# Token-stationary matmuls for the gates and the branch products of a hybrid decoder layer

## The chip, the cores and the metric

The kernel runs on one core of one Trainium2 chip. The metric is the time of one execution on the device, in microseconds. The names of the engines in the profile are PE for TensorE's matmuls, PEld for its weight loads (which overlap the matmuls), DVE for VectorE, ACT for ScalarE, POOL for GpSimd and SP for SyncE, whose queue issues most of the DMAs. All arithmetic is done in 32-bit floats.

## What is computed

The reference is one layer for 256 tokens of width 2048. Cut to what this change touches, it reads:

```python
proj = x @ w_in                      # (256 x 2048) @ (2048 x 14,352); columns are split among the mixers
y_lru = rg_lru(...)                  # 256 x 1024
y_gla = rmsnorm(gla(...)) * silu(r)                  # r: 1024 columns of proj
y_dn  = rmsnorm(gated_deltanet(...)) * silu(z)       # z: 1024 columns of proj
gates = sigmoid(gate_logits.reshape(256, 3, 2048) + b_gate)     # 6144 columns of proj
merged = (gates[:, 0] * (y_lru @ w_branch[0]) + gates[:, 1] * (y_gla @ w_branch[1])
          + gates[:, 2] * (y_dn @ w_branch[2]))      # w_branch[b]: 1024 x 2048
x = LN(alpha * x + merged @ w_out)                   # w_out: 2048 x 2048
x = LN(alpha * x + relu(x @ w1 + b1)**2 @ w2 + b2)   # w1: 2048 x 8192, w2: 8192 x 2048
```

The change concerns r, z, the gate logits, the three branch products and the way that merged reaches the product with w_out.

## The kernel before

Each large product is computed to nearly full precision from three passes of a reduced 32-bit type: every operand is split into hi (ACT casts it) and lo = raw - hi (DVE subtracts, `split`, lines 93 to 96), and the sum hi·hi + hi·lo + lo·hi is accumulated in PSUM.

The work is a list of jobs (`run_jobs`). A job is one block of weights of 1 MB (128 x 2048 numbers; 512 KB for a branch product): its DMA on SP into one of three `raw` buffers, its split into `hi` and `lo` halves (three buffers of each), its matmuls, and the evacuation of the sums. Load and split of a job are written ahead of the matmuls of the job before it.

There are two forms of matmul. In the first (`jobB`, `mmB`, lines 121 to 140, and `job_branch`), a 128 x 128 tile of weights is the stationary operand and the 256 tokens are the moving one; the sum has channels in rows and is 128 x 256. A job of 16 contraction tiles has 48 such matmuls, a branch job 24. In the second (`jobs_gla_v`, `jobs_out`, the second MLP product), 128 tokens are stationary and 512 columns of weights move; the sum has tokens in rows and is 128 x 512. A job has 24 such matmuls.

The gate jobs (line 124 onwards, 16 for each branch b) and the branch jobs (lines 982 to 986, 16 for each) alternate; `evac_gate` applies tanh on ACT, `evac_branch` multiplies on DVE and adds into `mg` on POOL (line 882). `mg` has channels in rows, as the output projection (`jobs_out`, lines 915 to 917) wants it for its stationary operand, so that it is only split into `mh` and `ml`.

Beside the jobs run the mixers, written as generators (`gen_lru`, `gen_gla`, `gen_dn` and others): after each job `pump` takes steps from them up to a budget of DVE and ACT time. `gen_dn` inverts triangular matrices through a round trip in DRAM on POOL's DMA queue. A scheduler then sets the order of the instructions on each engine from data dependences; each engine runs its own list in that order. After the output projection the first layer norm is computed (`norm_stats`, lines 944 to 947), transposed on PE (`p_x`, line 1077) and fed to the first MLP product (`accH`, then `accB` of lines 124 to 127 again).

PSUM has four buffers for the jobs' sums (`mm`) and four for the mixers (`mx`).

## Time and profile before

| | before |
|---|---|
| three timed runs | 1744.10, 1744.58 (median), 1745.21 us |
| span of the profiled execution, first to last instruction | 1743.0 us |
| mean granted TensorE clock | 0.997 |
| instructions | 30,261 |
| DMA | 319.96 MB, mean 184 GB/s |

The time of the profiled execution as a whole is not listed apart; its span lies 1.1 to 2.2 us under the three runs, 1.58 us under their median. In the profile, the duration of a matmul reaches from its start to the modelled end of its drain, so that matmuls that follow each other overlap; the pace is read from the distance of two starts. A row "A <- B" says that A waited for B. The granted clock 1.00 is the upper of TensorE's two levels.

### The profile page before, as it was taken

How to read it: one execution, taken by the hardware profiler on the slowest of the kernel's cores; microseconds unless marked ns; L12 is line 12 of the kernel's file. 1: busy time of each engine (PE TensorE's matmuls, PEld its weight loads, DVE VectorE, ACT ScalarE, POOL GpSimd, SP SyncE). 2: the span in 40 equal slices, each digit the busy share in tenths (PEclk: the TensorE clock that was granted, in tenths of full speed). 3: DMA queues.
4: the chain of work that ended last, by engine and by line, in shares of the span. 5: the costliest groups of instructions: out<-in, count | busy, mean ns of one | idle time of the engine just before them, and what ended most of it. 6: DMA issues, size and time to landing. Idle time of an engine off the chain costs nothing.

```text
span 1743.0 us, 30261 instructions
## 1 busy us (share of the span) xinstructions
PE 1722.7 (99%) x12782; PEld 1644.9 (94%) x12782; DVE 1058.2 (61%) x1353; ACT 889.8 (51%) x1209; POOL 76.7 (4%) x112
## 2 busy tenths in 40 slices
PE   8999999999999999999999999999999999999997
PEld 8999898999999999999998899999999988888897
DVE  7876456876765585565555675444444455576767
ACT  6785445785344443444444455554545444455553
POOL 0000000000120203000000000000000000000000
PEclk9999999999999999999999999999999999999999
DMA  8445543444564446355566835555545455555552
GB/s 328 150 170 187 197 173 125 166 170 149 184 194 148 161 170 187 130 181 182 184 217 223 308 109 209 190 177 187 187 177 193 172 192 195 194 193 193 203 193 97
DMA packets 52536, 319.96 MB, mean 184 GB/s; under 512 B 6752, under 2 KB 7136, under 8 KB 18992
## 3 DMA queue, kind: packets, MB, share of 16 engines
q1 hardware_dynamic: 49280, 310.92, 50.3%
q0 software_dynamic: 2976, 6.84, 1.5%
q8 instruction: 100, 1.64, 0.4%
q14 instruction: 36, 0.29, 0.0%
q10 hardware_dynamic: 144, 0.26, 0.0%
HBM read 315.09 MB, written 2.88 MB: 182 GB/s over the span
## 4 chain that ended last, share of the span: by engine, by line
PE 97%; DVE 1%; DMA 1%; ACT 0%; issue 0%; SPq 0%; DVEq 0%
PE accB L124 19%; PE accB L127 19%; PE accB L125 19%; PE accM L1200 7%; PE accM L1201 7%; PE accM L1199 7%; PE accB L982 3%; PE accB L984 3%; PE accB L986 3%; PE accO L917 1%; PE accO L915 1%; PE accO L916 1%; PE accV L467 1%; PE accV L469 1%; PE accV L468 1%; DMA raw<-in_w_dram 0%
## 5 line engine op out<-in xcount | busy, mean ns | idle before, releaser
L95 DVE TENSOR_TENSOR lo<-raw,hi 128x1024 fp32r<-128x1024 f32 (+2 forms) x584 | 708.6, 1216 | 541.6 <-ACT hi L94 537.8
L94 ACT CAST hi<-raw 128x1024 fp32r<-128x1024 f32 (+2 forms) x584 | 602.4, 1034 | 757.1 <-PE accB L125 406.0
L124 PE MATMUL accB<-xh,hi 128*128 128x256 f32 x1744 | 431.0, 285 | 0.0
L125 PE MATMUL accB<-xl,hi 128*128 128x256 f32 x1744 | 427.9, 283 | 0.0
L124 PEld LDWEIGHTS accB<-xh,hi 128*128 128x128 f32 x1744 | 334.4, 192 | 2.4 <-issue 1.4
L125 PEld LDWEIGHTS accB<-xl,hi 128*128 128x128 f32 x1744 | 334.5, 192 | 0.4
L127 PE MATMUL accB<-xh,lo 128*128 128x256 f32 x1744 | 244.9, 283 | 0.0
L124 PE MATMUL accB<-x1h,hi 128*128 128x256 f32 x976 | 239.7, 283 | 0.0
L125 PE MATMUL accB<-x1l,hi 128*128 128x256 f32 x976 | 239.5, 283 | 0.0
L127 PEld LDWEIGHTS accB<-xh,lo 128*128 128x128 f32 x1744 | 225.0, 192 | 0.1
L1200 PE MATMUL accM<-hi,hl 128*128 128x512 f32 (+1 forms) x608 | 212.8, 350 | 0.0
L1199 PE MATMUL accM<-hi,hh 128*128 128x512 f32 (+1 forms) x608 | 212.8, 350 | 0.0
L1201 PE MATMUL accM<-lo,hh 128*128 128x512 f32 (+1 forms) x608 | 212.8, 350 | 0.0
L125 PEld LDWEIGHTS accB<-x1l,hi 128*128 128x128 f32 x976 | 187.4, 192 | 0.0
L124 PEld LDWEIGHTS accB<-x1h,hi 128*128 128x128 f32 x976 | 187.4, 192 | 0.0
L127 PE MATMUL accB<-x1h,lo 128*128 128x256 f32 x976 | 137.0, 283 | 0.0
L1199 PEld LDWEIGHTS accM<-hi,hh 128*128 128x128 f32 x608 | 115.1, 189 | 15.1
L1200 PEld LDWEIGHTS accM<-hi,hl 128*128 128x128 f32 x608 | 115.1, 189 | 15.0
L1201 PEld LDWEIGHTS accM<-lo,hh 128*128 128x128 f32 x608 | 115.1, 189 | 14.8
L127 PEld LDWEIGHTS accB<-x1h,lo 128*128 128x128 f32 x976 | 125.9, 192 | 0.0
L982 PE MATMUL accB<-yh,hi 128*128 128x256 f32 x384 | 109.8, 286 | 0.0
L986 PE MATMUL accB<-yh,lo 128*128 128x256 f32 x384 | 108.7, 283 | 0.0
(308 smaller groups left out, 1861.3 us busy)
## 6 DMA issues: line engine op xcount, KB each, us to landing
raw<-in_wB_dram SPq DMA_DIRECT2D x109, 1024.0 KB, 4.8
raw<-in_w_dram SPq DMA_DIRECT2D x64, 1024.0 KB, 4.8
raw<-in_w2a_dram SPq DMA_DIRECT2D x32, 1024.0 KB, 4.8
raw<-in_w2b_dram SPq DMA_DIRECT2D x32, 1024.0 KB, 4.8
raw<-in_wBr_dram SPq DMA_DIRECT2D x48, 512.0 KB, 3.4
raw<-in_wO_dram SPq DMA_DIRECT2D x16, 1024.0 KB, 4.9
raw<-in_wV_dram SPq DMA_DIRECT2D x8, 1024.0 KB, 4.8
raw<-in_xw_dram SPq DMA_DIRECT2D x15, 384.0 KB, 8.0
```

What stands on the lines that cost most here:

```text
L94: i1 = sc.copy(hi, raw)
L95: i2 = ve.tensor_tensor(lo, raw, hi.bitcast(F32), ALU.subtract)
L124: te.matmul(acc, lhsT=hi[:, k, :], rhs=rh[:, k, :], start=start and k == 0, stop=False)
L125: te.matmul(acc, lhsT=hi[:, k, :], rhs=rl[:, k, :], start=False, stop=False)
L127: te.matmul(acc, lhsT=lo[:, k, :], rhs=rh[:, k, :], start=False, stop=stop and k == 7)
L467: te.matmul(accs[nh][tt], lhsT=sh, rhs=hi, start=k == 0, stop=False)
L982: te.matmul(acc[:, :T], lhsT=job.hi[0][:, 4 * i + k, :], rhs=yh[b][i][:, k, :], start=i == 0 and k == 0, stop=False)
L984: te.matmul(acc[:, :T], lhsT=job.hi[0][:, 4 * i + k, :], rhs=yl[b][i][:, k, :], start=False, stop=False)
L986: te.matmul(acc[:, :T], lhsT=job.lo[0][:, 4 * i + k, :], rhs=yh[b][i][:, k, :], start=False, stop=i == 1 and k == 3)
L1199: te.matmul(t, lhsT=sh, rhs=hi, start=k == 0, stop=False)
L1200: te.matmul(t, lhsT=sl, rhs=hi, start=False, stop=False)
L1201: te.matmul(t, lhsT=sh, rhs=lo, start=False, stop=k == NK2 - 1)
```

## The change

Five groups of products take the second form: r (`accR`), z (`accZ`), the gate logits (`accG`) and the branch products (`accY`) join `accV` in one function, `jobs_tok`. For each branch b and block cb of 512 channels there are now four gate jobs and two branch jobs, each of 1 MB. The sums have tokens in rows, so the gate's bias differs along a row: it is fetched as a row, broadcast to 128 partitions by POOL's DMA queue (`load_bg`, one buffer), and added on DVE before the tanh. `mg` has tokens in rows, and `gen_merged` transposes it on PE, 32 transposes of 128 x 128 in all (`p_m`), before ACT and DVE split it. silu(r) and silu(z) are multiplied in before the transposes that the mixers had already; ACT then scales and casts straight from PSUM (`to_branch_scaled`). The activation `dummy`, which loads the table for the square root ahead of the norm, now reads the row of biases instead of `mg`. A branch of 16 gate and 16 branch jobs becomes 16 gate and 8 branch jobs.

```diff
@@ -330,6 +327,10 @@
+    def to_branch_scaled(src, g, hi, lo):
+        sc.activation(hi, src, AF.Copy, scale=g)
+        ve.scalar_tensor_tensor(lo, src, g, hi.bitcast(F32), ALU.mult, ALU.subtract)
...
         ve.scalar_tensor_tensor(dst, t, 1.0, acc, ALU.add, ALU.mult)
 
-    def evac_gla_r(k):
-        def f(acc):
-            if k % 4 == 0:
-                gla["r", k // 4] = b4_tile("rr", [P, 4, T])
-            silu2(acc, gla["r", k // 4][:, k % 4, :])
-            if k == 7:
-                live.append(gen_gla())
+    def jobs_tok(src, nkg, rows_of, evac, nm):
+        accs = []
+        jobs = []
+        for kg in range(nkg):
+            job = Job(src[kg], 16, None, None)
+            def mm(job=job, kg=kg):
+                if kg == 0:
+                    accs.extend(mm_tile(nm) for _ in range(NT))
+                for k4 in range(4):
+                    k = 4 * kg + k4
+                    hi = job.hi[k4 // 2].rearrange("p k c -> p (k c)")[:, (k4 % 2) * 512:(k4 % 2) * 512 + 512]
+                    lo = job.lo[k4 // 2].rearrange("p k c -> p (k c)")[:, (k4 % 2) * 512:(k4 % 2) * 512 + 512]
+                    rh, rl = rows_of(k)
+                    for tt in range(NT):
+                        sh, sl = rh[:, tt * P:(tt + 1) * P], rl[:, tt * P:(tt + 1) * P]
+                        te.matmul(accs[tt], lhsT=sh, rhs=hi, start=k == 0, stop=False)
+                        te.matmul(accs[tt], lhsT=sl, rhs=hi, start=False, stop=False)
+                        te.matmul(accs[tt], lhsT=sh, rhs=lo, start=False, stop=k == 4 * nkg - 1)
+                if kg == nkg - 1:
+                    for tt in range(NT):
+                        evac(tt, accs[tt])
+            job.mm = mm
+            jobs.append(job)
+        return jobs
+    def x_rows(k):
+        return xh[k // 8][:, k % 8, :], xl[k // 8][:, k % 8, :]
+    def evac_gla_v(nh):
+        def f(tt, acc):
+            if nh == 0:
+                gla["v", tt] = b4_tile(f"v{tt}", [P, 4, 256])
+            (sc.copy if tt else ve.tensor_copy)(
+                gla["v", tt].rearrange("p h c -> p (h c)")[:, nh * 512:(nh + 1) * 512], acc)
         return f
 
-    def jobs_gla_v():
...
+    def evac_silu(dic, nm, nh, after=None):
+        def f(tt, acc):
+            if nh == 0:
+                dic[nm, tt] = b4_tile(nm, [P, 1024])
+            t = t2_tile("th", [P, 512])
+            sc.activation(t, acc, AF.Tanh, scale=0.5)
+            ve.scalar_tensor_tensor(dic[nm, tt][:, nh * 512:(nh + 1) * 512], t, 1.0, acc, ALU.add, ALU.mult)
+            if nh == 1 and tt == NT - 1 and after:
+                live.append(after())
+        return f
 
     def gen_gla():
         yield None
...
@@ -552,8 +563,9 @@
         y_alloc(1)
         for h in range(4):
             for tt in range(NT):
-                ve.tensor_scalar(o[tt][:, h, :], o[tt][:, h, :], rs[:, tt, h:h + 1], None, ALU.mult)
-            yield (.6, 0)
+                ve.scalar_tensor_tensor(o[tt][:, h, :], o[tt][:, h, :], rs[:, tt, h:h + 1],
+                                        gla["r", tt][:, h * 256:(h + 1) * 256], ALU.mult, ALU.mult)
+            yield (.8, 0)
         yield None
         for h in range(4):
             p = mx_tile("p_got")
...
-                ve.scalar_tensor_tensor(y, p[:, a * T:(a + 1) * T], g4[:, a:a + 1], gla["r", k // 4][:, k % 4, :],
-                                        ALU.mult, ALU.mult)
-                to_branch(y, yh[1][k // 4][:, k % 4, :], yl[1][k // 4][:, k % 4, :])
-            yield (1.8, .9)
-    dn = {"qk": {}, "z": {}, "v": {}, "nv": 0}
+                to_branch_scaled(p[:, a * T:(a + 1) * T], g4[:, a:a + 1],
+                                 yh[1][k // 4][:, k % 4, :], yl[1][k // 4][:, k % 4, :])
...
@@ -840,6 +843,9 @@
         for tt in range(NT):
             ve.tensor_tensor(o[tt], o[tt], rs[:, tt, :].unsqueeze(2).to_broadcast([P, 8, P]), ALU.mult)
             yield (1.1, 0)
+            ov = o[tt].rearrange("p h c -> p (h c)")
+            ve.tensor_tensor(ov, ov, dn["dz", tt], ALU.mult)
+            yield (1.1, 0)
         yield None
         for hp in range(4):
             p = mx_tile("p_dot")
...
-                                        ALU.mult, ALU.mult)
-                to_branch(y, yh[2][k // 4][:, k % 4, :], yl[2][k // 4][:, k % 4, :])
-            yield (1.4, .9)
-    mg = []
+                to_branch_scaled(p[:, j * T:(j + 1) * T], g4[:, 2:3],
+                                 yh[2][k // 4][:, k % 4, :], yl[2][k // 4][:, k % 4, :])
+            yield (1, .9)
...
+    mg = {}
     mh, ml = [], []
-    def evac_gate(b, d):
-        def f(acc):
-            t = t1_tile("gate", [P, T])
-            sc.activation(t, acc, AF.Tanh, scale=0.5, bias=bgh[:, b * 16 + d:b * 16 + d + 1])
-            gates[b, d] = t
+    gates = {}
+    def load_bg(b, cb):
+        t = sm.tile([P, 512], F32, tag="bg", name="bgrow", bufs=1)
+        gp.dma_start(t, bg[b:b + 1, cb * 512:(cb + 1) * 512].to_broadcast([P, 512]))
+        gates["row"] = t
+    def evac_gate(b, cb):
+        def f(tt, acc):
+            t = t2_tile("gate", [P, 512])
+            ve.tensor_tensor(t, acc, gates["row"], ALU.add)
+            sc.activation(t, t, AF.Tanh, scale=0.5)
+            gates[tt] = t
         return f
 
-    gates = {}
-    def evac_branch(b, d):
-        def f(acc):
-            i, j = d // 4, d % 4
-            if b == 0 and d == 0:
-                mg.extend(b4_tile(f"mg{a}", [P, 4, T]) for a in range(4))
-            m = mg[i][:, j, :]
-            t = gates.pop((b, d))
+    def evac_branch(b, cb):
+        def f(tt, acc):
+            if b == 0 and cb % 2 == 0:
+                mg[tt, cb // 2] = b4_tile(f"mg{tt}", [P, 1024])
+            m = mg[tt, cb // 2][:, (cb % 2) * 512:(cb % 2) * 512 + 512]
+            t = gates.pop(tt)
             if b == 0:
                 ve.scalar_tensor_tensor(m, t, 1.0, acc, ALU.add, ALU.mult)
                 return
-            u = t1_tile("gb", [P, T])
-            ve.scalar_tensor_tensor(u, t, 1.0, acc, ALU.add, ALU.mult)
-            gp.tensor_tensor(m, m, u, ALU.add)
-            if b == 2 and j == 3:
-                mh.append(b4_tile(f"mh{i}", [P, 4, T], F32R))
-                ml.append(b4_tile(f"ml{i}", [P, 4, T], F32R))
-                to_branch(mg[i], mh[i], ml[i])
+            ve.scalar_tensor_tensor(t, t, 1.0, acc, ALU.add, ALU.mult)
+            gp.tensor_tensor(m, m, t, ALU.add)
+            if b == 2 and tt == NT - 1:
+                live.append(gen_merged(cb))
         return f
 
+    def gen_merged(cb):
+        mh.append(b4_tile(f"mh{cb}", [P, 4, T], F32R))
+        ml.append(b4_tile(f"ml{cb}", [P, 4, T], F32R))
+        yield None
+        for kp in range(2):
+            p = mx_tile("p_m")
+            for a in range(2):
+                c = (cb % 2) * 512 + (2 * kp + a) * P
+                for tt in range(NT):
+                    te.transpose(p[:, a * T + tt * P:a * T + (tt + 1) * P], mg[tt, cb // 2][:, c:c + P], ident)
+            pv = p.rearrange("p (a t) -> p a t", a=2)
+            hi, lo = mh[cb][:, 2 * kp:2 * kp + 2, :], ml[cb][:, 2 * kp:2 * kp + 2, :]
+            sc.copy(hi, pv)
+            ve.tensor_tensor(lo, pv, hi.bitcast(F32), ALU.subtract)
+            yield (.7, .7)
     xt = {}
@@ -963,44 +984,35 @@
         jobs.append(jobB(wB[17 + h], evac_gla_q(h)))
     for h in range(4):
         jobs.append(jobB(wB[21 + h], evac_gla_k(h)))
-    jobs += jobs_gla_v()
-    for k in range(8):
-        jobs.append(jobB(wB[25 + k], evac_gla_r(k)))
+    for nh in range(2):
+        jobs += jobs_tok(wV[nh], 4, x_rows, evac_gla_v(nh), "accV")
+    for nh in range(2):
+        jobs += jobs_tok(wR[nh], 4, x_rows, evac_silu(gla, "r", nh, gen_gla), "accR")
     for h in range(8):
-        jobs.append(jobB(wB[33 + 8 + h], evac_dn("k", h)))
-        jobs.append(jobB(wB[33 + h], evac_dn("q", h)))
+        jobs.append(jobB(wB[25 + 8 + h], evac_dn("k", h)))
+        jobs.append(jobB(wB[25 + h], evac_dn("q", h)))
     for h in range(8):
-        jobs.append(jobB(wB[33 + 16 + h], evac_dn("v", h)))
-    def job_branch(b, d):
...
+        jobs.append(jobB(wB[25 + 16 + h], evac_dn("v", h)))
+    def y_rows(b):
+        return lambda k: (yh[b][k // 4][:, k % 4, :], yl[b][k // 4][:, k % 4, :])
+    hooks = {}
     for b in range(3):
-        for d in range(16):
-            jobs.append(jobB(wB[65 + b * 16 + d], evac_gate(b, d)))
-            jobs.append(job_branch(b, d))
+        for cb in range(4):
+            hooks[len(jobs)] = lambda b=b, cb=cb: load_bg(b, cb)
+            jobs += jobs_tok(wG[b, cb], 4, x_rows, evac_gate(b, cb), "accG")
+            if (b, cb) == (2, 0):
+                hooks[len(jobs)] = finish
+            jobs += jobs_tok(wBr[b, cb], 2, y_rows(b), evac_branch(b, cb), "accY")
         if b == 0:
-            for k in range(8):
-                jobs.append(jobB(wB[57 + k], evac_dn_z(k)))
+            for nh in range(2):
+                jobs += jobs_tok(wZ[nh], 4, x_rows, evac_silu(dn, "dz", nh), "accZ")
     n_mix = len(jobs)
     jobs += jobs_out()
 
     def run_jobs(js, hooks=()):
-        """Jobs in order; the split of a job stands before the mixers' steps of the one before it."""
         for i, job in enumerate(js):
             for nxt in js[i:i + 2]:
...
@@ -1015,16 +1027,15 @@
                 pump(0.6, 1.0)
 
     def before_out():
-        finish()
         dummy = sm.tile([P, 1], F32, tag="dummy", name="dummy", bufs=1)
-        sc.activation(dummy, mg[3][:, 3, 0:1], AF.Sqrt, scale=0.0, bias=eps[:, 3:4])
+        sc.activation(dummy, gates["row"][:, 0:1], AF.Sqrt, scale=0.0, bias=eps[:, 3:4])
         for tt in range(NT):
             st[tt] = sm.tile([P, 8, 6], F32, tag="bn", name="bn", bufs=2)
             for i in range(2):
                 xt[tt, i] = b4_tile(f"xt{tt}{i}", [P, 1024])
                 nc.sync.dma_start(xt[tt, i], xtok[tt * P:(tt + 1) * P, i * 1024:(i + 1) * 1024])
 
...
-    run_jobs(jobs, {0: load_consts, 1: load_wab, n_mix - 31: finish, n_mix: before_out, n_mix + 8: prep_first, n_mix + 15: finish})
+    hooks.update({0: load_consts, 1: load_wab, n_mix: before_out, n_mix + 2: finish, n_mix + 8: prep_first,
+                  n_mix + 15: finish})
+    run_jobs(jobs, hooks)```

How the order on the engines moves is shown at three places. The first is on PE, where the first gate product of the list ends and the first branch product begins (`yh`, `yl`: the branch's hi and lo; `p_E`, `p_kk`: steps of gen_dn). Before:

```order
L124 MATMUL accB_4628<-xh1_76,hi_4561 128x256
L125 MATMUL accB_4628<-xl1_78,hi_4561 128x256
L127 MATMUL accB_4628<-xh1_76,lo_4562 128x256 x8
L665 MATMUL p_E_4679<-gUh_4551,SLr_413 128x512
L666 MATMUL p_E_4679<-gUl_4552,SLr_413 128x512
L676 MATMUL p_kk_4686<-qk0_2767 128x256 x2
L676 MATMUL p_kk_4693<-qk1_3107 128x256 x2
L982 MATMUL accB_4710<-yh0_0_1383,hi_4624 128x256
L984 MATMUL accB_4710<-yl0_0_1385,hi_4624 128x256
L986 MATMUL accB_4710<-yh0_0_1383,lo_4625 128x256
```

The same engine and place now:

```order
L459 MATMUL accG_4408<-hi_4515,xh1_76 128x512
L460 MATMUL accG_4408<-hi_4515,xl1_78 128x512
L461 MATMUL accG_4408<-lo_4516,xh1_76 128x512
L459 MATMUL accG_4409<-hi_4515,xh1_76 128x512
L460 MATMUL accG_4409<-hi_4515,xl1_78 128x512
L461 MATMUL accG_4409<-lo_4516,xh1_76 128x512
L459 MATMUL accY_4628<-hi_4566,yh0_0_1381 128x512
L460 MATMUL accY_4628<-hi_4566,yl0_0_1383 128x512
L461 MATMUL accY_4628<-lo_4567,yh0_0_1381 128x512
L459 MATMUL accY_4629<-hi_4566,yh0_0_1381 128x512
```

Where one sum of 256 columns was built, two sums of 512 columns are built side by side, one for each half of the tokens, and a weight tile of 512 columns serves three matmuls of each.

The second place is on PE, where the output projection begins (`mh`, `ml`: merged, hi and lo). Before:

```order
L982 MATMUL accB_10282<-yh2_1_8341,hi_10217 128x256
L984 MATMUL accB_10282<-yl2_1_8343,hi_10217 128x256
L986 MATMUL accB_10282<-yh2_1_8341,lo_10218 128x256
L915 MATMUL accO_10336<-hi_10274,mh0_9158 128x512
L916 MATMUL accO_10336<-hi_10274,ml0_9159 128x512
L917 MATMUL accO_10336<-lo_10275,mh0_9158 128x512
```

Now, 24 matmuls of the projection later:

```order
L937 MATMUL accO_8027<-hi_7970,ml0_7295 128x512
L938 MATMUL accO_8027<-lo_7971,mh0_7294 128x512
L903 MATMUL p_m_8052<-ct_408,mg0_5237 128x128
L903 MATMUL p_m_8052<-ct_408,mg1_5239 128x128
L903 MATMUL p_m_8052<-ct_408,mg0_5237 128x128
L903 MATMUL p_m_8052<-ct_408,mg1_5239 128x128
L903 MATMUL p_m_8059<-ct_408,mg0_5237 128x128
L903 MATMUL p_m_8059<-ct_408,mg1_5239 128x128
L903 MATMUL p_m_8059<-ct_408,mg0_5237 128x128
L903 MATMUL p_m_8059<-ct_408,mg1_5239 128x128
L936 MATMUL accO_8026<-hi_8006,mh1_7530 128x512
```

The eight transposes of the last block of merged stand after the first job of the projection; those of the three blocks before stand in the same way after the first gate job of the next block.

The third place is on DVE, at the end of the output projection (`bn`, `mv`: the norm's statistics; `xt00` is the first half of the first 128 tokens, `xt11` the second half of the last 128). Before:

```order
L944 BN_AGGR mv_11026<-bn_10326 128x2
L946 RECIPROCAL mv_11026<-mv_11026 128x1
L921 SCALAR_TENSOR_TENSOR xt11_10334<-xt11_10334,accO_10803 128x256
L947 SCALAR_TENSOR_TENSOR mv_11026<-mv_11026 128x1
L1069 TENSOR_SCALAR xt00_10327<-xt00_10327,mv_11026 128x512
L923 BN_STATS bn_10331<-xt11_10334 128x6
L921 SCALAR_TENSOR_TENSOR xt11_10334<-xt11_10334,accO_10805 128x256
L923 BN_STATS bn_10331<-xt11_10334 128x6
L944 BN_AGGR mv_11031<-bn_10331 128x2
```

Now:

```order
L965 BN_AGGR mv_8730<-bn_8016 128x2
L942 SCALAR_TENSOR_TENSOR xt11_8024<-xt11_8024,accO_8507 128x256
L944 BN_STATS bn_8021<-xt11_8024 128x6
L967 RECIPROCAL mv_8730<-mv_8730 128x1
L942 SCALAR_TENSOR_TENSOR xt11_8024<-xt11_8024,accO_8509 128x256
L968 SCALAR_TENSOR_TENSOR mv_8730<-mv_8730 128x1
L1082 TENSOR_SCALAR xt00_8017<-xt00_8017,mv_8730 128x512
L944 BN_STATS bn_8021<-xt11_8024 128x6
L965 BN_AGGR mv_8735<-bn_8021 128x2
```

The reciprocal of the first half's norm stands behind a further evacuation and its statistics, and the scaling of `xt00` behind the second.

## Rows read from the trace of the kernel before

**Rows 1.** cores: span from first to last instruction, mean granted TensorE clock
```profile
core 0: 1743.0 us, clock 0.997
```

**Rows 2.** engines of the page: busy us (share of the span) x instructions
```profile
PE 1722.7 (99%) x12782; PEld 1644.9 (94%) x12782; DVE 1058.2 (61%) x1353; ACT 889.8 (51%) x1209; POOL 76.7 (4%) x112
```

**Rows 3.** page, chain that ended last, by engine
```profile
PE 97%; DVE 1%; DMA 1%; ACT 0%; issue 0%; SPq 0%; DVEq 0%
```

**Rows 4.** waits of PE: engine, line, waited for: us in total, times, longest
```profile
PE acc L189 <- ACT hi L94: 4.2, 2, 3.8
PE p_x L1077 <- DVE xt L1069: 2.0, 1, 2.0
PE accO L917 <- DVE lo L95: 1.3, 1, 1.3
```

**Rows 5.** windows: stretch, us, busy (x records) by engine, PEclk, DMA share, GB/s
```profile
160.40:203.90 43.50, 43.50 (x194) 36.04 (x193) 21.30 (x20) 16.59 (x17) 0.00 (x0) 1.00 0.53 192
411.00:570.00 159.00, 159.00 (x1328) 157.38 (x1327) 100.03 (x162) 66.68 (x100) 21.29 (x30) 1.00 0.52 174
...
1020.00:1376.00 356.00, 356.00 (x2969) 356.00 (x2968) 166.36 (x144) 181.54 (x257) 1.62 (x3) 1.00 0.51 182
1377.00:1550.00 173.00, 173.00 (x766) 143.28 (x765) 96.60 (x96) 83.61 (x97) 0.00 (x0) 1.00 0.54 194
```

**Rows 6.** timeline of PE, gate stage: start us, us, engine line op
```profile
799.76 0.28 PE L124 MATMUL accB<-xh,hi 128*128 128x256 f32 x1
...
803.00 0.28 PE L125 MATMUL accB<-xl,hi 128*128 128x256 f32 x1
```

**Rows 7.** timeline of PE, branch product, transposes, next gate
```profile
743.33 0.28 PE L982 MATMUL accB<-yh,hi 128*128 128x256 f32 x1
...
744.65 0.28 PE L986 MATMUL accB<-yh,lo 128*128 128x256 f32 x1
744.77 0.60 PE L848 MATMUL p_dot<-ct,do 128*128 128x128 f32 x4
745.12 0.36 PE L124 MATMUL accB<-xh,hi 128*128 128x256 f32 x1
745.32 0.28 PE L125 MATMUL accB<-xl,hi 128*128 128x256 f32 x1
```

**Rows 8.** tile accV: duration ns min/median/max, first and last start
```profile
L467 PE MATMUL accV<-hi,xh x64: 389/389/396, 160.4 to 203.3; 128*128 128x512 f32 x64
...
L469 PE MATMUL accV<-lo,xh x64: 389/389/389, 160.9 to 203.7; 128*128 128x512 f32 x64
```

**Rows 9.** timeline of PE, start of the output projection
```profile
910.64 0.40 PE L915 MATMUL accO<-hi,mh 128*128 128x512 f32 x1
...
912.03 0.39 PE L915 MATMUL accO<-hi,mh 128*128 128x512 f32 x1
```

**Rows 10.** timeline of PE, transposes of the first norm
```profile
1003.45 2.85 PE L1077 MATMUL p_x<-ct,xt 128*128 128x128 f32 x16 [2.01 <-DVE xt L1069]
```

**Rows 11.** tile accO on DVE: duration ns min/median/max, first and last start
```profile
L921 DVE SCALAR_TENSOR_TENSOR xt<-xt,accO x10: 401/674/689, 929.9 to 1000.8; 128x512 f32<-128x512 f32 x6, 128x256 f32<-128x256 f32 x4
```

**Rows 12.** tile EU on POOL, same columns
```profile
L670 POOL TENSOR_TENSOR EU<-E,ct x4: 1331/1336/1835, 418.1 to 594.4; 128x512 f32<-128x512 f32 x4
```

**Rows 13.** line L882 on POOL, same columns
```profile
L882 POOL TENSOR_TENSOR mg<-mg,gb x32: 727/742/2785, 628.0 to 911.4; 128x256 f32<-128x256 f32 x32
```

**Rows 14.** timeline of DVE, first norm
```profile
999.54 0.16 DVE L946 RECIPROCAL mv<-mv 128x1 f32<-128x1 f32 x1 [0.36 <-ACT mv L945]
...
999.62 0.40 DVE L921 SCALAR_TENSOR_TENSOR xt<-xt,accO 128x256 f32<-128x256 f32 x1
...
1000.47 0.42 DVE L923 BATCH_NORM_STATS2 bn<-xt 128x6 f32<-128x256 f32 x1
```

**Rows 15.** timeline of ACT, dummy's table load, first norm
```profile
913.28 1.28 ACT L1020 ACT_TABLE_LOAD   x1
...
999.22 0.29 ACT L945 ACTIVATE mv<-mv,eps 128x1 f32<-128x1 f32 x1 [6.16 <-DVE mv L944]
```

More of the change, by code (lines that the diff above doesn't have):

```diff
@@ L34 @@
 C_DN_G = C_GLA_G + 2
-C_BG = C_DN_G + 1
-C_B1 = C_BG + 48
+C_B1 = C_DN_G + 1
 C_G1 = C_B1 + 64
@@ L65, in trunk_kernel @@
 @with_exitstack
-def trunk_kernel(ctx, tc, xw, xtok, par, lat, con, wab, wa2, wB, wV, wBr, wO, w1, w2a, w2b, rows, out):
+def trunk_kernel(ctx, tc, xw, xtok, par, lat, con, wab, wa2, wB, wV, wR, wZ, wG, wBr, wO, w1, w2a, w2b, rows, bg, out):
     nc = tc.nc
@@ L972, in trunk_kernel @@
     for h in range(8):
-        jobs.append(jobB(wB[33 + 16 + h], evac_dn("v", h)))
-    def job_branch(b, d):
-        job = Job(wBr[b, d], 8, None, None)
-        def mm():
-            acc = mm_tile("accB")
-            for i in range(2):
-                for k in range(4):
-                    te.matmul(acc[:, :T], lhsT=job.hi[0][:, 4 * i + k, :], rhs=yh[b][i][:, k, :],
-                              start=i == 0 and k == 0, stop=False)
-                    te.matmul(acc[:, :T], lhsT=job.hi[0][:, 4 * i + k, :], rhs=yl[b][i][:, k, :],
-                              start=False, stop=False)
-                    te.matmul(acc[:, :T], lhsT=job.lo[0][:, 4 * i + k, :], rhs=yh[b][i][:, k, :],
-                              start=False, stop=i == 1 and k == 3)
-            evac_branch(b, d)(acc[:, :T])
-        job.mm = mm
-        return job
@@ L1268, in lay_out @@
     small[:, R_A:R_A + 8] = da
-    wB = np.concatenate([tiles(t) for t in (small, lx, ly, gq, gk, gr, qkv, dz, gl)], 0)
-    wBr = np.stack([tiles(f["w_branch"][b]) for b in range(3)], 0)
+    wB = np.concatenate([tiles(t) for t in (small, lx, ly, gq, gk, qkv)], 0)
+    wG = np.stack([blocks(gl[:, b * D:(b + 1) * D], 4, 512) for b in range(3)], 0)
+    wBr = np.stack([blocks(f["w_branch"][b], 4, 512) for b in range(3)], 0)
     def ch(v):
```

52 lines of the change are left out of this document (8 added, 44 removed).

## The prediction

> **What bounds the kernel now.** I read the cores first: one core, span 1743.0 us, granted clock 0.997 [rows 1], so nothing is to be explained or won by the clock. Then the engines: PE is covered for 99% of the span by matmuls, DVE for 61%, ACT for 51% [rows 2]. A covered PE may still wait between pipelined matmuls, so the next two views decide: the chain of waits that ended last lies on PE for 97% [rows 3], and the list of PE's waits holds 7.5 us in all, none of them between the first inputs and the output projection [rows 4]. The windows say the same by stage: PE is busy without a gap in the projections, the gates and the MLP, while DVE is at 63% in the first gate stage (100.03 of 159.00) and the DMA engines at 0.52 [rows 5]. So in the stages that change, the time is the sum of PE's starts, and what DVE, ACT, POOL and DMA do counts only if it comes late.
>
> The last thing to read is PE's pace in its two forms. Weights stationary, 256 tokens moving: from 799.76 to 803.00 there are 27 starts, 0.1200 us each [rows 6]; in a branch product 11 starts from 743.33 to 744.65, 0.1200 too [rows 7]. Tokens stationary, 512 columns moving: 64 matmuls on each of three lines start between 160.4 and 203.7, 191 distances of 0.2267 us [rows 8]. Two of the first do the work of one of the second: 0.2400 against 0.2267 us. PEld shows the same from the other side: it is busy 356.00 of 356.00 us in the first form and 36.04 of 43.50 in the second [rows 5], for a loaded tile now serves twice the columns.
>
> **The change part by part.**
>
> *The matmuls.* Gate logits 48 x 48 = 2304, branch products 48 x 24 = 1152, r and z 8 x 48 = 384 each: 4224 matmuls of 256 columns become 2112 of 512. All of them lie on the path. 4224 x 0.1200 = 506.9 us; 2112 x 0.2267 = 478.8 us; 28.1 us go. The bounds: the slowest pace that the rows show for 512 columns is that of the first six distances of the output projection, 910.64 to 912.03, 0.2317 us [rows 9], with which 17.5 us go. The fastest is the second MLP product, 173.00 us for 766 records, 0.2258 [rows 5] (records can be missing, so this is an upper bound of the pace), with which 30.0 go. I take 0.2267, since accV has the operands of the new jobs, x stationary and blocks of 1 MB, and lies beside the same mixers.
>
> A rule speaks against this. The Trainium skill, TensorE: Matmul & The Clock Gate, section Back-to-back issue gap, gives the warm distance of two matmuls as their columns at 2.4 GHz plus about 2.5 ns, 109.2 ns for 256 and 215.8 for 512 columns. By that rule a pair would save 2.5 ns, 5.3 us in all, and the sum below would come out at 1743.5 us. The rows do not agree: at 2.4 GHz, the level of the granted clock of 1.00, the columns alone take 106.7 and 213.3 ns, and the distance is 13 ns longer at both sizes.
>
> *The transposes of merged.* 32 new ones on PE, in groups of four. Four of the kind take 0.35 us, 744.77 to 745.12, and the matmul behind them starts its follower 0.08 us late (0.20 for 0.12) [rows 7]: 0.43 x 8 = 3.4 us. Bounds: without the delay 32 x 0.0875 = 2.8; by the batch of 16 in 2.85 us [rows 10], drain included, 5.7. They wait for merged: behind the last matmul of a block DVE has two products of at most 0.69 us [rows 11], then POOL two additions of 128 x 512, for which its product of that shape took 1.34 us [rows 12]: 4.1 us in all. The cover is the job that the order puts between, 24 matmuls or 5.4 us, with 1.3 us to spare. POOL's additions of half the size have a median of 0.74 us, but reached 2.79 [rows 13]; two of twice that, 11.2 us, and DVE's 1.4 less the cover of 5.4 would hold PE for 7 us at one of the four blocks. I take 0, by the median, and keep one such block for the range.
>
> *Evacuation, biases, splits.* Per block a gate now costs DVE an addition and ACT a tanh twice, a branch costs DVE a product twice; DVE's four take at most 4 x 0.69 = 2.8 us [rows 11] where four products of about 0.4 us stood. They lie beside PE. A sum has four PSUM buffers, so the next block's gate waits only if the gate before it is not emptied by the end of its branch jobs, 10.9 us later. The split of a job stands in DVE's order a job ahead of its matmuls, so an evacuation has 5.4 us to get out of its way; in the projection, where each block's evacuation is longer (two products of 0.69 us and four statistics), PE waited once, 1.3 us [rows 4]. The row of biases goes through POOL's queue, behind gen_dn's DMAs that wait for DVE; it is asked for four jobs, 21.8 us, ahead. The same weights are loaded, now in 5.4 us for each MB instead of 5.8; accV and the second MLP product ran so at DMA shares of 0.53 and 0.54 without a wait of PE [rows 5]. I cost all this at 0.
>
> *The first norm.* A product (0.40 us) and a statistics instruction (0.42 us) now stand ahead of the reciprocal [rows 14], and PE sits idle until that norm is applied, 2.01 us before its 16 transposes [rows 10]. So up to 0.8 us is added; I take 0.8, with 0 as the lower bound. The table for the square root: dummy no longer waits for merged and runs ahead of the last tanh, so that the table is loaded again, and a third time before the norm's first square root, 1.28 us each [rows 15]. ACT sat idle for 6.16 us there [rows 15], and the load itself waits for nothing: 0.
>
> *Sum.* -28.1 + 3.4 + 0.8 = -23.9 us: a span of 1719.1 us. The span lay 1.58 us under the median of the runs, which gives **1720.7 us**.
>
> **The rivals.**
>
> *Late splits (smaller gain).* DVE's evacuations come in bursts of 1.4 us, at 28 places (12 gates, 12 branches, 4 for r and z), with gen_dn's steps between. For it: DVE rises from 63% as PE gets shorter, and mixer steps end sooner and closer together. Against it: no such wait at 411 to 570 us, nor in accV. With 0.3 us at each place: 1720.7 + 8.4 = 1729.1 us.
>
> *A slower pace for 512 columns.* Were the 0.2317 us of rows 9 the rule beside busy DMA and DVE, the gain would be 17.5 - 4.2 = 13.3 us: 1731.3 us. Against it: six distances there, 191 in accV.
>
> *No gain from the form.* If beside the mixers a matmul of 512 columns took as long as two of 256, 0.2400 us, only the transposes and the norm would be left: 1744.6 + 4.2 = 1748.8 us. Against it: the slowest pace in the rows is 0.2317. The rule of the Trainium skill named above comes out near it, at 1743.5 us.
>
> *Slower.* The same evacuations hold PE at each of the 28 places for as long as the one wait of the projection, 1.3 us: 36.4 us, hence 1757.1 us. It decides from 23.9 / 28 = 0.85 us at each place on. It would take DVE falling behind by a whole job, which its 63% does not suggest.
>
> That the change does not do what it says is excluded by the order on PE, where the 512-column matmuls and the transposes stand.
>
> **How the numbers follow.** The forecast, 1717.5 to 1725 us, has 0.74; late splits 0.12; the slower pace 0.06; no gain 0.02; slower 0.04; a larger gain (pace 0.2258, the least for the transposes and the norm: 30.0 - 2.8 = 27.2 us, 1717.4 us, and under) 0.02. The range, 1716 to 1732 us, holds the forecast, the late splits and the slower pace, and leaves out the upper ends of the bounds taken together (17.5 - 5.7 - 7 - 0.8 = 4 us of gain, 1740.6 us). Runs of this kernel tell a change from none at 0.2%, 3.5 us: faster 0.94 (the forecast, both smaller gains, the larger one), the same 0.01 and slower 0.05 (no gain counts half to each, beside the slower case).
>
> **What would show it.** In the profile of the changed kernel: distances of 0.227 us in accR, accZ, accG and accY, at a granted clock of 1.00; 2112 fewer matmuls of these groups, and 32 of p_m with no wait of PE for mg; no line of PE waiting for lo, hi or an evacuation between 30 us and the end of the projection; the output projection beginning some 25.5 us earlier than at 910.64 (28.1 less three of four blocks of transposes, 2.6); and PE's wait for xt before the norm's transposes grown from 2.0 to 2.8 us. The forecast falls if PE waits for lo or for a PSUM buffer at the gates' evacuations, if POOL's additions run at several times 1.34 us, or if the pace lies above 0.230.

## The result and the profile after

| | before | after |
|---|---|---|
| median of four runs each | 1744.34 us (1743.48 to 1745.21) | 1726.51 us (1725.34 to 1727.16) |
| ratio, 95% interval | | 0.9899 [0.9885, 0.9913] |
| span of the profiled execution | 1743.0 us | 1723.6 us |
| instructions | 30,261 | 25,980 |
| DMA | 319.96 MB | 322.80 MB |

The change takes away 17.8 us. Forecast were 23.9 us (1720.7), with a range of 1716 to 1732 us. The sign, the mechanism and the range held; 6 us of the gain did not appear, and most of what follows looks for them. 1726.5 us also lies above the 1717.5 to 1725 us to which the forecast gave 0.74: it is inside the range only because that was kept wide for late splits and a slower pace.

The engines of the profile after, busy us (share of the span) x instructions, against [rows 2]:

```profile
PE 1699.3 (99%) x10702; PEld 1537.1 (89%) x10702; DVE 1064.1 (62%) x1334; ACT 887.6 (51%) x1183; POOL 86.2 (5%) x108
```

2080 PE records fewer (2112 matmuls less, 32 transposes more), PE still covered, DVE where it was. The five longest waits of PE after, against [rows 4] (engine, tile, line, waited for: us in total, times, longest):

```profile
PE acc L188 <- ACT hi L93: 7.1, 2, 3.9
PE p_x L1090 <- DVE xt L1082: 1.3, 1, 1.3
PE p_x L1090 <- issue: 1.1, 1, 1.1
PE accO L938 <- DVE lo L94: 1.0, 1, 1.0
PE p_i L740 <- DVE q L733: 1.0, 1, 1.0
```

Nothing waits for an evacuation, for merged or for a PSUM buffer, and the wait for lo at the start of the projection stood there before (1.3 us). But the first line, the wait for the very first inputs, has grown from 4.2 to 7.1 us, in a stretch whose matmuls the change does not touch; the norm's one wait of 2.0 us has become two, of 1.3 and 1.1; and the last line is new.

Windows after, against [rows 5]: accV, accR, the first gate and branch stage with LRU, accZ (stretch, us, busy x records for PE, PEld, DVE, ACT, POOL, then PEclk, DMA share, GB/s):

```profile
164.50:208.00 43.50, 43.50 (x194) 36.05 (x193) 21.30 (x20) 16.59 (x17) 0.00 (x0) 1.00 0.54 192
208.00:251.50 43.50, 43.50 (x193) 36.03 (x193) 21.15 (x19) 20.12 (x21) 0.00 (x0) 1.00 0.56 194
412.50:562.00 149.50, 149.50 (x734) 124.79 (x733) 100.44 (x160) 63.66 (x90) 23.80 (x34) 1.00 0.55 181
562.20:610.00 47.80, 47.80 (x213) 39.71 (x212) 28.89 (x49) 19.64 (x22) 11.52 (x14) 1.00 0.55 182
```

r now takes the same 43.5 us for 192 matmuls as v did, and PEld is idle for a sixth of the gate stage, where before it was covered for 157.38 of 159.00 us. The branch products and the new transposes, on PE's timeline (start us, us, line, out<-in, shapes):

```profile
439.62 0.39 PE L459 MATMUL accY<-hi,yh 128*128 128x512 f32 x1
...
443.02 0.39 PE L459 MATMUL accY<-hi,yh 128*128 128x512 f32 x1
...
796.22 0.39 PE L461 MATMUL accG<-lo,xh 128*128 128x512 f32 x1
796.45 1.03 PE L903 MATMUL p_m<-ct,mg 128*128 128x128 f32 x8
797.24 0.48 PE L459 MATMUL accG<-hi,xh 128*128 128x512 f32 x1
797.55 0.40 PE L460 MATMUL accG<-hi,xl 128*128 128x512 f32 x1
```

From 439.62 to 443.02 there are 15 distances, 0.2267 us each, the pace forecast from [rows 8]. Eight transposes take 0.79 us (796.45 to 797.24), and the distance behind them is 0.31 instead of 0.23.

To see where the 6 us are, I cut each trace at two places that the change does not move: the first start of accV, ahead of all changed products, and the first start of accO, behind them.

| trace | start to accV | accV to accO | accO to the end |
|---|---|---|---|
| before | 160.4 | 750.2 | 832.3 |
| after | 164.5 | 727.1 | 832.0 |
| difference | +4.1 | -23.1 | -0.4 |
| forecast | 0 | -25.5 | +1.7 |

These are single traces; their spans lie 19.4 us apart, the medians 17.8. So 4.1 us are lost before the first changed matmul, and 2.4 in the stages that change; 2.1 are given back in the end. The start, on ACT's timeline of after:

```profile
3.20 0.40 ACT L93 CAST xh<-raw 128x256 fp32r<-128x256 f32 x1 [1.17 <-DMA raw<-in_xw_dram]
...
9.13 0.40 ACT L93 CAST xh<-raw 128x256 fp32r<-128x256 f32 x1 [4.86 <-DMA raw<-in_xw_dram]
```

and on POOL's:

```profile
1.37 0.71 POOL L868 DMA_DIRECT2D bgrow<-in_bg_dram  x1 [0.43 <-issue]
```

The second slice of x is cast at 9.13 us, after ACT has sat idle for 4.86 us until its DMA landed. At 1.37 us POOL had issued the first row of biases, 256 KB in SBUF, that nothing reads before 439 us. That made theory S: the row's load competes with the first slices. Its rivals: the start differs from build to build (V), or POOL's queue costs whenever it runs (Q).

### The profile page after: what moved, and what is told of

Read it like the earlier page. It is cut to its first block, busy times and chain, and to the rows that moved or that the text cites. A ratio compares the mean times of both kernels' runs of the same rounds, so it can differ in the third digit from the quotient of the medians.

```text
span 1723.6 us, 25980 instructions
## 1 busy us (share of the span) xinstructions
PE 1699.3 (99%) x10702; PEld 1537.1 (89%) x10702; DVE 1064.1 (62%) x1334; ACT 887.6 (51%) x1183; POOL 86.2 (5%) x108
## 4 chain that ended last, share of the span: by engine, by line
PE 98%; DVE 1%; DMA 0%; ACT 0%; issue 0%; SPq 0%; DVEq 0%
PE accB L123 12%; PE accB L126 12%; PE accB L124 12%; PE accM L1212 7%; PE accM L1214 7%; PE accM L1213 7%; PE accG L460 5%; PE accG L461 5%; PE accG L459 5%; PE accY L461 3%; PE accY L460 3%; PE accY L459 3%; PE accO L938 2%; PE accO L937 2%; PE accO L936 2%; PE accZ L459 1%
## 5 line engine op out<-in xcount | busy, mean ns | idle before, releaser
L94 DVE TENSOR_TENSOR lo<-raw,hi 128x1024 fp32r<-128x1024 f32 (+2 forms) x584 | 706.1, 1212 | 569.9 <-ACT hi L93 557.3
L93 ACT CAST hi<-raw 128x1024 fp32r<-128x1024 f32 (+2 forms) x584 | 603.4, 1036 | 734.4 <-PE accB L124 223.1
L124 PE MATMUL accB<-x1l,hi 128*128 128x256 f32 x976 | 239.5, 283 | 0.0
L124 PEld LDWEIGHTS accB<-x1l,hi 128*128 128x128 f32 x976 | 187.4, 192 | 0.0
L123 PE MATMUL accB<-xh,hi 128*128 128x256 f32 x720 | 178.3, 285 | 0.0
L124 PE MATMUL accB<-xl,hi 128*128 128x256 f32 x720 | 176.5, 283 | 0.0
L459 PE MATMUL accG<-hi,xh 128*128 128x512 f32 x384 | 150.9, 393 | 0.0
L460 PE MATMUL accG<-hi,xl 128*128 128x512 f32 x384 | 149.9, 390 | 0.0
L461 PE MATMUL accG<-lo,xh 128*128 128x512 f32 x384 | 149.8, 390 | 0.0
L123 PEld LDWEIGHTS accB<-xh,hi 128*128 128x128 f32 x720 | 137.9, 191 | 2.1 <-issue 1.4
L124 PEld LDWEIGHTS accB<-xl,hi 128*128 128x128 f32 x720 | 138.0, 192 | 0.3
L126 PE MATMUL accB<-xh,lo 128*128 128x256 f32 x720 | 101.1, 283 | 0.0
```

Of the source, the lines that this page charges most:

```text
L93: i1 = sc.copy(hi, raw)
L94: i2 = ve.tensor_tensor(lo, raw, hi.bitcast(F32), ALU.subtract)
L123: te.matmul(acc, lhsT=hi[:, k, :], rhs=rh[:, k, :], start=start and k == 0, stop=False)
L124: te.matmul(acc, lhsT=hi[:, k, :], rhs=rl[:, k, :], start=False, stop=False)
L126: te.matmul(acc, lhsT=lo[:, k, :], rhs=rh[:, k, :], start=False, stop=stop and k == 7)
L459: te.matmul(accs[tt], lhsT=sh, rhs=hi, start=k == 0, stop=False)
```

## The experiments

All times are medians on one chip for each group, beside runs of the kernel before. Each of these kernels was also cut at the two places:

| kernel | time, kernel before | ratio, 95% interval | start to accV | accV to accO | accO to the end |
|---|---|---|---|---|---|
| after, again | 1727.46, 1743.68 | 0.9909 [0.9895, 0.9922] | 165.0 | 727.1 | 833.9 |
| 1 first row on SP | 1723.48, 1743.10 | 0.9893 [0.9878, 0.9909] | 161.7 | 727.1 | 832.8 |
| 2 first row held back | 1721.75, 1743.10 | 0.9876 [0.9863, 0.9890] | 160.0 | 727.1 | 832.9 |
| 2 again | 1722.56, 1743.60 | 0.9878 [0.9864, 0.9891] | 162.2 | 727.1 | 832.1 |
| 3 before + early row | 1747.66, 1743.10 | 1.0026 [1.0016, 1.0035] | 164.1 | 750.2 | 829.5 |
| 4 before + early block | 1747.37, 1743.10 | 1.0025 [1.0014, 1.0035] | 165.8 | 750.2 | 830.5 |
| 5 transposes twice | 1729.51, 1743.68 | 0.9922 [0.9909, 0.9934] | 165.1 | 729.7 | 832.7 |
| 6 r and z back | 1730.79, 1743.68 | 0.9931 [0.9918, 0.9945] | 165.1 | 731.1 | 834.4 |
| 7 gate's addition twice | 1729.86, 1743.68 | 0.9925 [0.9912, 0.9937] | 165.2 | 730.6 | 832.4 |
| 8 mixers 1.2 | 1722.52, 1743.60 | 0.9876 [0.9860, 0.9891] | 161.6 | 725.7 | 832.8 |
| 9 mixers 0.6 | 1730.92, 1743.60 | 0.9925 [0.9913, 0.9938] | 162.1 | 732.5 | 835.2 |

The last three columns come from one trace of each. The middle one repeats to 0.1 us wherever the middle is unchanged, so differences of 1 us can be read there that the total does not tell.

**After, again.**

> The kernel after, unchanged, run again beside the experiments of this group. Every theory expects its ratio to the kernel before again, 0.990 (1726.5 us where the kernel before takes 1744.3), with accV beginning at 164 to 165 us.

It came as expected: 0.9909, accV at 165.0 us.

**1. The first row through SP.**

```diff
-        gp.dma_start(t, bg[b:b + 1, cb * 512:(cb + 1) * 512].to_broadcast([P, 512]))
+        (gp if b or cb else nc.sync).dma_start(t, bg[b:b + 1, cb * 512:(cb + 1) * 512].to_broadcast([P, 512]))
```

> The kernel after, with its first row of biases loaded through SP's queue, behind the third block of weights, instead of through POOL's at 1.4 us; the other eleven rows stay on POOL, and PE, DVE and ACT have the same order. Theory S (the first row's broadcast competes with the first slices of x and weights): PE's second wait at the start falls from 3.28 to some 0.3 us, accV begins at 160.4 instead of 164.5 us, and the time falls by 4.1 us, 1726.5 to 1722.4. Rival V (the start differs from build to build, whatever the first row does): accV stays at 164 to 165 us, 1726.5 us.

accV began at 161.7 us, 2.8 to 3.3 earlier than in the two traces of after; the time, 19.6 us under the kernel before, stands between the two forecasts, with one run of four at 1727.3 us. SP issued the row at 41.70 us, so the queue and the moment are both changed here; the next experiment changes the moment alone.

**2. The first row later, on the same queue.**

```diff
         t = sm.tile([P, 512], F32, tag="bg", name="bgrow", bufs=1)
+        if (b, cb) == (0, 0):
+            gp.tensor_tensor(t[:, :T], zs, zs, ALU.add)
         gp.dma_start(t, bg[b:b + 1, cb * 512:(cb + 1) * 512].to_broadcast([P, 512]))
```

> The kernel after, with the first row still on POOL's queue, but made to wait: POOL first writes a part of its tile from zs, which DVE has ready only at some 30 us. Theory S: as with the row on SP, accV at 160.4 us and 1722.4 us, for it is the moment of the load that counts. Rival Q (rows on POOL's queue cost, whenever they run, for instance because that queue's packets are slow): a part of the loss stays, accV at 162 us or later; 1724 to 1726.5 us. Rival V: 1726.5 us.

Its timeline on POOL, then on ACT:

```profile
29.11 0.71 POOL L869 TENSOR_TENSOR bgrow<-zs 128x256 f32<-128x256 f32 x1 [28.17 <-DVE zs L241]
30.13 0.73 POOL L870 DMA_DIRECT2D bgrow<-in_bg_dram  x1 [0.31 <-POOL bgrow L869]
```
```profile
5.99 0.41 ACT L93 CAST xh<-raw 128x256 fp32r<-128x256 f32 x1 [1.66 <-DMA raw<-in_xw_dram]
```

The same load at 30.13 instead of 1.37 us; the second slice is cast at 5.99 instead of 9.13 us, accV begins at 160.0, and the ratio is 0.9876. Run again in another group it gave 0.9878:

> The kernel with the first row of biases held back on POOL's queue (the version of the experiment before), unchanged, beside the next two. Its ratio to the kernel before should come again: 0.988, some 21.3 us less.

Q falls: the queue is the same, only the moment differs. V falls as the cause of the loss, for accV begins at 164.1 to 165.8 us in all seven traces with an early load and at 160.0 to 162.2 in all five of after with the row moved. But a part of the start does differ by itself: the two traces of this version lie 2.3 us apart there (160.0 and 162.2), with the second slice cast at 5.99 and 6.61 us and PE's starts 0.21 us apart until 8.1 and 12.6 us. This is the fastest version measured, 21.0 to 21.4 us under the kernel before.

**3. The same load put into the kernel before.**

```diff
-    gp.memset(eps[:, 3:4], LN_EPS)
-    bgh = const.tile([P, 48], F32, name="bgh")
+    gp.memset(eps[:, 3:4], LN_EPS); early = sm.tile([P, 512], F32, tag="early", name="early", bufs=1)
+    gp.dma_start(early, rows[0:1, 0:512].to_broadcast([P, 512])); bgh = const.tile([P, 48], F32, name="bgh")
```

> The kernel before, with one load more that nothing reads: a row of 512 numbers broadcast to 128 partitions (256 KB written) on POOL's queue, at the place where the kernel after has its first row of biases; every other order is unchanged. Theory S: the whole loss of the start appears in the kernel before, accV at 164.5 instead of 160.4 us, 1744.3 + 4.1 = 1748.4 us. Rival V: accV at 160.4 us, 1744.3 us.

1747.66 us, 4.6 more than the kernel before beside it. The window from 5 to 10 us of this kernel and of the version held back:

```profile
5.00:10.00 5.00, 1.84 (x10) 1.55 (x9) 0.55 (x2) 1.06 (x3) 0.00 (x0) 1.00 0.94 320
```
```profile
5.00:10.00 5.00, 4.98 (x29) 4.44 (x28) 2.94 (x6) 3.17 (x8) 0.00 (x0) 1.00 0.98 348
```

The DMA engines are as busy in the one as in the other (0.94 and 0.98); what they carry differs, and PE is busy for 1.84 instead of 4.98 us. The clock column reads 1.00 in both, but that does not fit the pace: at the beginning of these 5 us PE's starts of 256 columns lie 0.21 us apart in both kernels. They do so again in this one from 11.0 to 13.8 us, and there its next window has the clock:

```profile
10.00:15.00 5.00, 4.78 (x27) 4.57 (x28) 4.79 (x10) 4.13 (x10) 0.00 (x0) 0.66 1.03 410
```

256 columns in 0.213 us are 1.2 GHz, the lower of the two levels.

**4. The same bytes from 128 rows.**

```diff
-    gp.memset(eps[:, 3:4], LN_EPS)
-    bgh = const.tile([P, 48], F32, name="bgh")
+    gp.memset(eps[:, 3:4], LN_EPS); early = sm.tile([P, 512], F32, tag="early", name="early", bufs=1)
+    gp.dma_start(early, xtok[0:P, 0:512]); bgh = const.tile([P, 48], F32, name="bgh")
```

> The kernel before, with an unread load of the same 256 KB at the same place, but from 128 different rows of DRAM (a block of x) instead of one row read 128 times. Theory S1 (it is the bytes and packets that compete): the same loss as with the broadcast row, about +4 us, 1748.4 us. Theory S2 (reading one row 128 times is what slows the DMA engines): 256 KB at the 330 GB/s that the start moves is 0.8 us, and with PE's lower clock behind a longer wait 1 to 1.5 us: 1745.1 to 1745.8 us. Rival V: 1744.3 us.

1747.37 us, 4.3 more than before. S2 falls: a block of 128 different rows costs as much as one row read 128 times. Why 256 KB cost 3 us of waiting, where the some 330 GB/s of the first 20 us would carry them in 0.8, is settled only in part. In the first 10 us the early load takes 10.4 to 16.6% of the time of all 16 DMA engines (after again and after; 13.0% in experiment 3, 11.5% here), that is 1.0 to 1.7 us of all of them; the rest stays open.

**5. The transposes done twice.**

```diff
-                for tt in range(NT):
+                for tt in (0, 1, 0, 1):
                     te.transpose(p[:, a * T + tt * P:a * T + (tt + 1) * P], mg[tt, cb // 2][:, c:c + P], ident)
```

> The kernel after with each of the 32 transposes of merged done twice into the same place; nothing else is moved. Theory: they lie on PE's path at the 0.099 us that the trace of after shows for one (eight in 0.79 us), so the time rises by 32 x 0.099 = 3.2 us. Rival 1 (part of the group's time is hidden, for the next job would be held by its split or its evacuation anyway): 0 to 1.5 us. Rival 2 (the longer group also delays the copies out of PSUM and so the projection): over 5.7 us.

The total rose by 2.0 us only; the middle, which holds three of the four blocks, by 2.7 (2.4 by 24 x 0.099). So they lie on the path at their own duration. The rise of the total is smaller because of the projection's start: in their traces after again waited 1.5 us there for lo, this kernel didn't.

**6. r and z back in the first form** (the evacuations and the mixers' ends are those of the kernel before).

```diff
-    for nh in range(2):
-        jobs += jobs_tok(wR[nh], 4, x_rows, evac_silu(gla, "r", nh, gen_gla), "accR")
+    for k in range(8):
+        jobs.append(jobB(wR[k], evac_gla_r(k)))
...
-            for nh in range(2):
-                jobs += jobs_tok(wZ[nh], 4, x_rows, evac_silu(dn, "dz", nh), "accZ")
+            for k in range(8):
+                jobs.append(jobB(wZ[k], evac_dn_z(k)))
```

> The kernel after with r and z alone back in the first form (weights stationary, 256 tokens moving, channels in rows, silu multiplied in behind the mixers' transposes); gates, branches and merged stay as in after. Theory: 768 matmuls x 0.1200 = 92.2 us take the place of 384 x 0.2267 = 87.1 us, so 5.1 us more than after. Rival 1 (beside the mixers the wide form gains nothing): 0. Rival 2 (the wide form's bursts of evacuation and the mixers' steps cost PE something, which goes with it): 2 to 4 us more.

3.3 us in total, 4.0 in the middle: rival 2's figure. The waits of PE say what it is that goes with the wide form; there is no wait for q any more:

```profile
PE acc L188 <- ACT hi L93: 8.0, 2, 4.1
PE accO L954 <- DVE lo L94: 1.5, 1, 1.5
PE p_x L1106 <- DVE xt L1098: 1.3, 1, 1.3
PE p_x L1106 <- issue: 1.1, 1, 1.1
PE accO L952 <- ACT hi L93: 0.6, 1, 0.6
```

5.1 us by the pace less the 1.0 us of that wait is 4.1. PE's distances in the two middles say the same: 92.5 us for accB take the place of 87.5 for accR and accZ, and those of p_i fall by 1.1. Whether the wait belongs to the wide form or to the place of the mixers' steps is asked by experiment 8.

**7. The gates' addition twice**, 16.6 us more of DVE's time.

```diff
             ve.tensor_tensor(t, acc, gates["row"], ALU.add)
+            ve.tensor_tensor(t, acc, gates["row"], ALU.add)
             sc.activation(t, t, AF.Tanh, scale=0.5)
```

> The kernel after with DVE's addition of the biases done twice for every gate block, 24 x 0.69 = 16.6 us of DVE's time more, at the places where the evacuations stand; the result is the same. Theory: DVE's evacuations lie beside PE with slack, so the time stays within 1 us of after. Rival (late splits: the evacuation already holds the next job's split, and so PE): up to the whole 16.6 us, and at 0.3 us at each place 7.2 us.

2.4 us more than after again, past the 1 us of the theory and far from the rival's 7.2, with runs from 1727.5 to 1732.5 us. The trace has no wait for lo or hi among the gates, so late splits are not it. First PE's timeline in the matrix inversion, then two windows of the same trace:

```profile
678.88 2.05 PE L740 MATMUL p_i<-dD,q 128*128 128x128 f32 x16 [0.99 <-DVE q L733]
...
681.71 0.41 PE L750 MATMUL p_dt<-ct,dD 64*64 64x64 f32 x4 [0.44 <-DVE dD L742]
```
```profile
684.00:688.00 4.00, 4.00 (x19) 2.50 (x18) 1.75 (x4) 1.01 (x2) 3.07 (x3) 0.53 0.21 66
688.00:692.00 4.00, 4.00 (x26) 3.88 (x25) 1.33 (x5) 0.38 (x1) 0.00 (x0) 0.62 0.00 0
```

Behind two waits among small matmuls the granted clock is 0.53 and 0.62 of 2.4 GHz for 8 us: 8 x (1 - 0.575) = 3.4 us, nearly all of the middle's 3.5. The five runs follow their mean clock: 1727.52 us at 0.997, 1732.47 at 0.993. So the additions hold no job's matmuls; the time is lost in PE's chain with the mixers. DVE is not later there: its second product dD begins 2.09 us behind the step p_i in this trace as in that of after. But the edit moved PE's order: in after two matmuls of a gate job stand between the two groups of p_dt, here none, and PE waits 0.44 us. That this wait brought on the fall of the clock is likely but not shown.

**8 and 9. The mixers' steps spread again.** After a job, the mixers may use 2.0 us of DVE; after a branch job of the kernel before, half as wide, it was 0.6. The branch jobs of after are full jobs and get 2.0. In the trace of after at most 4 matmuls stand between the steps of the inversion from p_dt on, where the kernel before has 10 to 48. The theory was that PE so comes to a step before DVE has made its operand. On the version held back:

```diff
+            job.short = nkg == 2
...
-            if job.nk == 16:
+            if getattr(job, 'short', False):
+                pump(1.2, 2.0)
+            elif job.nk == 16:
                 pump(2.0, 2.2)
```

> The version with the first row held back, and after a branch job the mixers get 1.2 us of DVE's time instead of 2.0, so that two halves as wide as before give them together what a branch's jobs gave in the kernel before (16 x 2.0 + 8 x 1.2 = 41.6 us; after: 48). In PE's order the steps of the matrix inversion (p_i, p_dt, p_ks) then stand 16 to 24 matmuls apart instead of 1 to 3. Theory B (bunched steps of the mixers cost PE the wait for q, 1.0 us, and up to 1.6 us of gaps and delays around them): 1 to 2 us less than the version it is made from, and no wait of PE for q. Rival (the wait is the price of the wide evacuations on DVE, wherever the steps stand): no change within 0.5 us, and PE still waits for q.

> The same with 0.6 us of DVE's time after a branch job, the figure of the kernel before for one half as wide (36.8 us for a branch's jobs in all). The steps spread still further, but the last of them (p_dot) end only just ahead of the third branch. Theory B: as with 1.2, 1 to 2 us less. Rival (the mixers now end late, and PE waits for yh or yl of the third branch): 1 us or more slower than with 1.2.

With 1.2 the first steps still stand 1 to 3 matmuls apart, the later ones 16 to 24. The wait for q is gone; PE's waits are now

```profile
PE acc L188 <- ACT hi L93: 4.5, 2, 3.9
PE p_x L1095 <- DVE xt L1087: 1.3, 1, 1.3
PE p_x L1095 <- issue: 1.1, 1, 1.1
PE accO L941 <- DVE lo L94: 0.5, 1, 0.5
```

and the middle is 725.7 instead of 727.1 us: 1.4 less, as theory B has it. In the total it doesn't show (1722.52 and 1722.56 us; its runs reach from 1718.82 to 1724.13). But the wait for q, the larger part of it, is not a matter of the matmuls between the steps: the first two steps p_i follow each other without one in the kernel before too, and it does not wait. DVE's timeline of after has a split of the next job ahead of q:

```profile
676.48 1.23 DVE L94 TENSOR_TENSOR lo<-raw,hi 128x1024 fp32r<-128x1024 f32 x1 [1.49 <-PE p_i L730]
677.62 1.28 DVE L733 TENSOR_TENSOR q<-p_i,ct 128x512 f32<-128x512 f32 x2
```

q begins 2.19 us behind the start of that step (675.43), against 1.09 in the kernel before and with r and z back. With 1.2 it is 1.29, for there the split begins 0.15 us behind the start of the step, in after 1.05. With 0.6 (`pump(0.6, 1.0)`) its rival holds: the middle is 5.4 us longer than in the version held back, since the mixers end late.

```profile
PE p_dot L855 <- DVE do L848: 5.1, 2, 3.9
```

The wait is for o, ahead of the transposes that make yh and yl, and the clock falls behind it here too (window 780 to 790 us):

```profile
780.00:790.00 10.00, 10.00 (x43) 8.64 (x44) 4.95 (x10) 5.38 (x10) 0.00 (x0) 0.81 0.10 16
```

## Why the prediction was right, and where 6 us went

*The pace: right.* 0.2267 us per matmul in accR and accY, at a granted clock of 1.00. Summed over all distances of PE's starts between accV and accO, accB gives up 510.1 us and accR, accZ, accG and accY take 482.7: 27.4 us, where 28.1 were forecast. The difference is in the starts right behind a mixer's matmul, which are late by 3.9 us in all in the new form (482.7 less 2112 x 0.2267) and were by 3.2 in the old one. Experiment 6 prices a part of the change by time and agrees once the wait for q is set off. The fast bound of 0.2258 us was a misreading: the 766 records of that window count matmuls that began before it, 763 start in it, and its pace is 0.2267 too. The rule of the Trainium skill that was weighed (TensorE: Matmul & The Clock Gate, Back-to-back issue gap), by which the kernel was estimated at 1743.5 us, doesn't hold here: the distances are 120.0 and 226.7 ns, 13 ns over the columns at both sizes. That section of the Trainium skill gives it as the gap of an isolated matmul, not of a stream of weight loads and matmuls, which this kernel is.

*The transposes: right.* 2.4 us for three blocks, with 0.08 behind each; the two together are 0.87 for a block and 3.5 for four, against 3.4 forecast. Done twice they cost the same again. POOL never made them wait, as taken.

*Evacuation, biases, splits: the step that failed.* "I cost all this at 0" was true of the evacuations and of the splits as far as the jobs' own matmuls go, for which no trace lists a wait of PE between 30 us and the projection, and of eleven of the twelve rows. It was wrong of the first one. "it is asked for four jobs, 21.8 us, ahead" describes where the call stands in the program. But a load that depends on nothing isn't held by its place in the program: POOL had only its first constants to set before it, and issued it at 1.37 us. There it costs 3 us of waiting for the second slice, and 1 us more for the matmuls behind it, which run 0.21 us apart, the pace of the lower clock level, until 14.4 us, where in the kernel before this ended at 8.1 us. The step missing is to follow each added DMA to its place in its own queue and to look at what the other queues carry then. Taking the load away from there (experiments 1 and 2) and putting it into the kernel before (3 and 4) give 2 to 5 us: 1.8 to 3.4 and 3.2 to 5.1 by the gain beside the two measurements of after, 4.6 and 4.3 by the loss.

*The mixers: not priced.* That their steps would "end sooner and closer together" stood with the rival of late splits, as its cause, and no price was set on it in the sum. It costs 1.9 us: the wait of 1.0 for q, 0.7 of gaps in p_i, p_kk and p_dt, and 0.2 in the mixers' other matmuls. 27.4 us less the 2.4 of the transposes and these 1.9 are the 23.1 of the middle. Experiment 8 gets 1.4 back, nearly all of it in p_i, by moving them: the split then holds q for 0.2 us instead of 1.1. The gaps in p_kk and p_dt stay.

*The end: the sum right by luck.* +0.8 for the norm and 0.9 for the last block of transposes were forecast; the two first traces show -0.4. But this stretch differs from trace to trace: 832.3, 829.5 and 830.5 us in three traces of the kernel before (an early load at its start changes nothing here), 832.0, 833.9, 832.8, 832.9 and 832.1 in five of after and its versions with the first row moved. The means are 830.8 and 832.7, 1.9 more, but not by the terms of the sum. The norm was mis-sized: from the last start of accO to the first of accH lie 5.09 us in the two traces of the kernel before in which the clock stays at 1.00 there, and 5.19 in four of after (the first, and those of experiments 1, 2 and 2 again), 0.1 us more instead of 0.8. PE's timeline of after shows that wait in two pieces, against the one of 2.01 us in [rows 10]:

```profile
983.34 0.78 PE L1090 MATMUL p_x<-ct,xt 128*128 128x128 f32 x4 [1.09 <-issue]
985.42 1.53 PE L1090 MATMUL p_x<-ct,xt 128*128 128x128 f32 x12 [1.30 <-DVE xt L1082]
```

The rest lies in the projection: 89.1 us in the mean from its first to its last start before, 90.8 after, of which 0.9 are the transposes and most of the remainder is PE's wait for lo in the first job (0, 0.7 and 1.3 us before, 1.0 to 1.5 after). The clock behind the norm's wait moves single traces as well: 0.67 from 986 to 990 us in after again and 1.00 there in after, and 0.57 from 1004 to 1008 us in the trace of the kernel before.

With the first row held back the gain is 21.0 to 21.4 us; 1.9 of the mixers and 0.7 behind their matmuls make that 23.6 to 24.0 us, by addition the 23.9 of the forecast; no run shows it as a time, and totals of one kernel differ by 1 to 2 us.

*The rivals and the signs.* Late splits, the slower pace, no gain from the form and the slower case show in none of the traces ahead of the projection: between 30 us and there PE's only wait listed for after is the one for q. Of the signs, the pace, the counts and the transposes without a wait for mg came as named. The projection began 19.0 us earlier (910.64 to 891.60), not 25.5: 4.1 of the difference lie in the start, 2.4 in the middle. PE's waits ahead of the norm's transposes grew from 2.0 to 2.4 us, not 2.8. And the wait for lo in the projection (1.0 us), which the sign excluded, stood there in the kernel before (1.3).
